# Two-layer encoder on one core: square sums of the set-up taken by ScalarE from a second, token-major input copy, and the third weight pair loaded in the set-up

## The chip, the cores and the metric

One core of one Trainium2 chip runs the program. A core has TensorE (PE, matmuls, with a queue of weight loads, PEld), VectorE (DVE), ScalarE (ACT), GpSimd (POOL) and SyncE (SP), which here issues all DMAs. The metric is the device time of one execution in microseconds; of several executions the median counts.

## The reference, cut to what is computed

The input is 512 tokens of 1024 features, float32. Layer 0 mixes tokens by a gated delta rule (8 heads of 128), layer 1 by a gated linear recurrence, and each is followed by a squared-ReLU MLP with 4096 hidden features. Every part starts with an RMS norm over the features of a token:

```python
def _rmsnorm(x, w):
    xf = x.astype(jnp.float32)
    y = xf * lax.rsqrt(jnp.mean(xf * xf, axis=-1, keepdims=True) + EPS)
    return (y * w.astype(jnp.float32)).astype(x.dtype)
...
proj = y @ w_in                      # 1024 x 4112, split in q, k, v, gate, a, b
qkv = jax.nn.silu(_causal_conv(qkv, conv_w)).astype(f32)
```

The change concerns the first of these norms and the first projections.

## The kernel before

Activations lie feature-major: 8 tiles of 128 features x 512 tokens. A float32 product is made of rounded parts: each weight and each input is split in a high and a low part, and a block of 128 output features takes, for each of the 8 feature tiles k, three matmuls of 512 columns: whi with yh (L125), whi with yl (L126), wlo with yh (L127), 24 in all. Weights come in pairs of blocks, 1 MB of float32 ("raw", two buffers). ScalarE rounds raw to whi (L114) and a second engine subtracts to get wlo (L115). There are three sets of whi and wlo tiles; the third set has tags of its own.

The norm's factor is applied behind the projection: y is only x times the norm's weight, and a projected block is multiplied by the row factors rB afterwards (z, L389, for the heads). So TensorE can start before the square sums are there, and the first use of rB is after the first block.

`setup` (L230 to L262) runs over the feature tiles in steps that end at 1, 2, 4, 6, 8. Each step loads the x tiles (L267), splits each into yh (ScalarE, L216) and yl (VectorE, L219), takes its square on ScalarE (L160, L163) and adds it to the sum sqacc on VectorE or GpSimd (L165); then it loads the step's pieces of the first two weight pairs (L251) and splits them, the first pair's wlo on GpSimd and the second's on VectorE (L252). After the loop come constants, all on SP's queue.

`gdn` (L271 on) loads more constants and gdn_ab, the weights of the decay and gate columns, casts them (L286), and then asks for the first six projected blocks: `stream` makes the first four from the two pairs of the set-up with the loop over k outside (96 matmuls), then loads the third pair and projects its two blocks. With a raised priority, `rstd_rows` turns sqacc into rB: rounded high and low parts, two matmuls "ps" with a column of ones (L195), a wide scaling, Ln and Exp on 128x512, three wide VectorE passes. `gdn_decay` follows with pab (16 matmuls over all y, L335), pt, and small work. Another function, `rstd` (L167), which the second layer uses, goes by a 128x4 tile: small Ln, Exp and VectorE steps to the root rsr, then four broadcasts "pb" through TensorE (L180) and one copy to rB.

The order of the instructions on each engine is fixed when the program is built: a planner takes, by priority, what it reckons to be ready by its own estimate of times. On the chip each engine works through its order and waits where a result is late.

Of the kernel before, what the change touches and what calls it, by code (L numbers as in the profile page):

```python
# [11 lines left out]
F32 = mybir.dt.float32  # L12
F32R = mybir.dt.float32r
U8 = mybir.dt.uint8
AF = mybir.ActivationFunctionType
# [3 lines left out]
T, D, HID, NH, P = 512, 1024, 4096, 8, 128  # L19
NB = D // P  # L20
B = 32
MIX = {"ma": 2, "mb": 3}
NC = T // P
EPS = 1e-6
# [9 lines left out]
class Net:  # L34
# [59 lines left out]
        self.last_switch, self.since_switch = i, []  # L94


    def weight_tiles(self):
        tile = lambda tag, dt, bufs: self.wp.tile([P, NB, 256], dt, tag=tag, bufs=bufs, name=self.name(tag))
        self.nw_tiles += 1

        last = self.nw_tiles % 3 == 0 and not self.two
        return (tile("raw", F32, 2), *(tile(t + "3", F32R, 1) if last else tile(t, F32R, 2) for t in ("whi", "wlo")))

    def weights(self, src):

# [24 lines left out]
    def stream(self, src, y, first=None, wide=0, tokens=slice(0, T), spare=0):  # L130


        n = src.shape[0]
        if wide:
            first = first or [self.weights(src[i]) for i in range(wide)]
            yield from self.project([(w, b) for w in first for b in (0, 1)], y, tokens)
        for i in range(wide, n):
            w = self.weights(src[i])
            for b in (0, 1):
                yield self.project([(w, b)], y, tokens, i - wide < spare)[0]  # L140

# [22 lines left out]
            e = nc.gpsimd if eng == "g" else nc.vector  # L164
            e.tensor_tensor(out=self.sq, in0=self.sq, in1=t, op=ALU.add)  # L165

    def rstd(self):  # L167

        nc = self.nc
        ps = self.mix("ps")  # L170
        for c in range(NC):
            nc.tensor.matmul(ps[:, c:c + 1], lhsT=self.sq[:, c * P:(c + 1) * P], rhs=self.ones,
                             start=True, stop=True)
        x = self.work("rsx", [P, NC])
        nc.vector.tensor_scalar(out=x, in0=ps[:, 0:NC], scalar1=1.0 / D, scalar2=EPS,
                                op0=ALU.mult, op1=ALU.add)
        r = self.rsqrt(x, "rs")
        pb = self.mix("pb")
        for c in range(NC):
            nc.tensor.matmul(pb[:, c * P:(c + 1) * P], lhsT=r[:, c:c + 1].to_broadcast([P, P]),  # L180
                             rhs=self.ident, start=True, stop=True)
        rb = self.work("rB", bufs=2)
        nc.scalar.copy(out=rb, in_=pb)
        return r, rb
# [35 lines left out]
                                       op0=ALU.mult, op1=ALU.subtract)  # L220
        return yh, yl

    def renew(self, c, norm, sq_eng="g", act=False):

        with self.tc.high_priority(offset=3000 if c == NB - 1 else 0):
            self.y[c] = self.split_norm(c, self.nw[:, norm * NB + c:norm * NB + c + 1], act)
            self.square_into(c == 0, self.h[c], sq_eng)


    def setup(self, w):  # L230

        nc = self.nc
        self.table("natural_log_exp_and_others")
        self.h, self.y = [], [None] * NB

        zeros = self.work("gate", bufs=2)
        nc.vector.memset(zeros, 0.0)
        warm = self.mix("warm", [P, WARM])
        for _ in range(2):
            nc.tensor.matmul(warm, lhsT=zeros[:, 0:P], rhs=zeros[:, 0:WARM], start=True, stop=True)  # L240
        pairs = [self.weight_tiles() for _ in (0, 1)]
        start = 0
        for end in (1, 2, 4, 6, 8):
            k = slice(start, end)
            for c in range(start, end):
                self.h.append(self.load_x(c))
                if c == 0:
                    self.nw = self.const("norms", [P, 5 * NB])
                self.renew(c, 0, "g" if c % 2 or c == 0 else "v", act=True)
            for i, (raw, hi, lo) in enumerate(pairs):  # L250
                nc.sync.dma_start(out=raw[:, k], in_=w[i][:, k])  # L251
                self.split_weights(raw, hi, lo, k, (nc.gpsimd, nc.vector)[i])  # L252
            start = end
        self.ident = self.const("ident", [P, P])
        self.ones = self.const("ones", [P, 1])
        self.one = self.cp.tile([P, 1], F32R, tag="one", name="one")
        nc.scalar.copy(out=self.one, in_=self.ones)
        self.tri = self.work("e", [P, P])
        nc.sync.dma_start(out=self.tri, in_=self.a["tri"])
        self.lmask = self.mask("lmask", [P, len(LEVELS) + 1, B])  # L260
        self.ident32 = self.const("ident32", [P, B])
        return [(hi, lo) for _, hi, lo in pairs]  # L262

    def load_x(self, c):
        tag, bufs = (("kd", 3), ("aa", 3), ("n", 2))[c % 3]
# [5 lines left out]
    def gdn(self, first):  # L271
        nc, a = self.nc, self.a
        self.emask = self.const("emask", [P, P])
        self.conv = self.const("conv", [P, 3 * NH, 4])
        self.onorm = self.const("onorm", [P, 1])
        self.pick = self.const("pick", [4 * NH, 2 * NH])
        alog = self.cp.tile([P, NH], F32, tag="alog", name="alog")
        nc.sync.dma_start(out=alog, in_=a["alog"].partition_broadcast(P))
        dtb = self.cp.tile([P, NH], F32, tag="dtb", name="dtb")
        nc.sync.dma_start(out=dtb, in_=a["dtb"].partition_broadcast(P))  # L280

        abraw = self.work("gate", [P, NB, 2 * NH], bufs=2)
        nc.sync.dma_start(out=abraw, in_=a["gdn_ab"])
        ab = self.work("x", [P, NB, 4 * NH], F32R)
        hi = ab[:, :, 0:2 * NH]
        nc.scalar.copy(out=hi, in_=abraw)  # L286
        nc.vector.tensor_tensor(out=ab[:, :, 2 * NH:], in0=abraw, in1=hi.bitcast(F32), op=ALU.subtract)


        blocks = self.stream(a["gdn_in"][0:3 * NH // 2], self.y, first, 2, spare=1)  # L290
        blocks = chain([next(blocks) for _ in range(6)], blocks)
        with self.tc.high_priority(offset=3000):
            self.rb = self.rstd_rows()
            self.gdn_decay(ab, alog, dtb)


        self.two = True
        xa, xb = (self.wp.tile([P, 4, T], F32, tag=t, bufs=1, name=self.name(t)) for t in ("whi3", "wlo3"))
        self.extra = dict(kq=xa[:, 0:2], v=xa[:, 2], kd=xa[:, 3], aa=xb[:, 0], n=xb[:, 1], ot=xb[:, 2], w2=xb[:, 3])
        self.o, self.on = [None] * NH, [None] * NH  # L300
        hd = {0: self.gdn_conv(0, blocks)}
        self.gdn_silu([hd[0]])
        for j in range(NH + 2):
            todo = []
            if j + 1 < NH:
                hd[j + 1] = self.gdn_conv(j + 1, blocks)
                todo.append(hd[j + 1])
            sg = []
            for i in GATES[j]:
                sg += self.gdn_gates(i)  # L310
            with self.tc.high_priority(offset=3000):
                for i in SCANS[j]:
                    self.gdn_scan(i, hd)
                if j < NH:
                    self.gdn_local(j, hd)
                if 2 <= j <= NH and j % 2 == 0:
                    self.gdn_inverse((j - 2, j - 1), hd)
                if todo or sg:
                    self.gdn_silu(todo, sg)
            for h, t in sg:  # L320
                self.gdn_gated(h, t)
        self.nw_tiles, self.two = 0, False
        self.h = [self.load_x(c) for c in range(NB)]
# [656 lines left out]
def layout(x, gdn_w_in, gdn_conv, gdn_a_log, gdn_dt_bias, gdn_onorm, gdn_w_out, hgrn_w_in, hgrn_lb_logits,  # L980
           hgrn_gnorm, hgrn_w_out, norm_mix, norm_mlp, mlp_w_up, mlp_w_down, norm_final):
    i = np.arange(P)
    block = lambda start, h: np.arange(start + h * P, start + (h + 1) * P)
    o = {"x": x[0].T.reshape(NB, P, T).transpose(1, 0, 2)}
    norms = np.stack([norm_mix[0], norm_mlp[0], norm_mix[1], norm_mlp[1], norm_final])
    o["norms"] = norms.reshape(5, NB, P).transpose(2, 0, 1).reshape(P, 5 * NB)
    o["ident"] = np.eye(P, dtype=np.float32)
# [8 lines left out]
    w = gdn_w_in[0]  # L996
# [5 lines left out]
    w = hgrn_w_in[0]  # L1002
# [22 lines left out]
```

## Time and profile before

| | us |
|---|---|
| median of 3 runs (lowest, highest) | 1361.32 (1360.67, 1361.95) |
| the profiled execution | 1360.81 |
| its span, first to last instruction | 1359.0 |
| TensorE busy | 1332.3 |
| VectorE busy | 819.8 |
| ScalarE busy | 546.4 |
| GpSimd busy | 171.9 |
| mean granted TensorE clock | 0.994 |

The profile was taken in one execution; times in it count from the start of the span. A line of the timeline gives the start and duration of an instruction, and in brackets the idle time of its engine before it with what released it. Matmuls are pipelined, so the distance of two starts, not the duration, is what one costs. A clock of 1.00 is full speed, 0.50 the lower of the two levels. Some matmul records can be missing.

### The profile page before, as it was taken

To read this page: it belongs to the slowest core of one execution; us is meant where nothing else is said; L and a number is where in the kernel's file an instruction comes from. 1 tells how busy PE (TensorE), PEld (TensorE's weight loads), DVE (VectorE), ACT (ScalarE), POOL (GpSimd) and SP (SyncE) were. 2 spreads that over 40 slices of the span, in tenths; PEclk is the share of its full clock that TensorE was granted. 3 is DMA by queue.
4 is the path that set the end of the run, shared out by engine and by line. 5 is a ranking of instruction groups with operands and counts; after the bars stand their busy time and mean duration, and the time that the engine had idled before them with its cause. 6 is when DMAs were issued, how large, how long until landed. Compare 5 with 4: busy or idle time off the path is not lost.

```text
span 1359.0 us, 24194 instructions
## 1 busy us (share of the span) xinstructions
PE 1332.3 (98%) x10340; PEld 1101.3 (81%) x10340; DVE 819.8 (60%) x1408; ACT 546.4 (40%) x1016; POOL 171.9 (13%) x172
## 2 busy tenths in 40 slices
PE   7999999999999999999999999999999999999997
PEld 5777777878888888888888888888888888888897
DVE  5896777766844444444483997787674444445453
ACT  5663556454344224132123444545334313214242
POOL 4001021100200120201220010100100020110232
PEclk8999999999999999999999999999999999999999
DMA  6131111222332222232320211121142223232242
GB/s 200 42 115 35 61 64 34 79 79 66 136 109 94 93 93 93 94 102 94 114 93 31 95 64 64 63 94 63 62 155 93 93 94 110 93 108 93 93 140 78
DMA packets 23356, 121.57 MB, mean 89 GB/s; under 512 B 3664, under 2 KB 6864, under 8 KB 9680
## 3 DMA queue, kind: packets, MB, share of 16 engines
q1 hardware_dynamic: 23248, 120.02, 26.2%
q8 instruction: 81, 1.33, 0.4%
q14 instruction: 27, 0.22, 0.0%
HBM read 117.91 MB, written 2.10 MB: 88 GB/s over the span
## 4 chain that ended last, share of the span: by engine, by line
PE 87%; DVE 6%; ACT 4%; issue 1%; DMA 0%; POOL 0%; SPq 0%; POOLq 0%; DVEq 0%; ACTq 0%
PE pj L126 25%; PE pj L125 25%; PE pj L127 25%; PE pga L475 1%; DVE whi L739 1%; PE pj L712 1%; PE pj L711 1%; PE pj L710 1%; ACT whi L114 1%; PE gr L780 1%; PE pu L520 1%; PE px L513 1%; DVE wlo L115 1%; PE pw L590 1%; PE po L826 1%
## 5 line engine op out<-in xcount | busy, mean ns | idle before, releaser
L114 ACT CAST whi<-raw 128x1024 fp32r<-128x1024 f32 (+2 forms) x222 | 221.2, 1023 | 416.0 <-PE pj L126 400.9
L115 DVE TENSOR_TENSOR wlo<-raw,whi 128x1024 fp32r<-128x1024 f32 (+2 forms) x217 | 290.9, 1352 | 153.0 <-ACT whi L114 150.7
L126 PE MATMUL pj<-yl,whi 128*128 128x512 f32 x960 | 382.3, 398 | 0.0
L125 PE MATMUL pj<-yh,whi 128*128 128x512 f32 x960 | 381.2, 397 | 0.8 <-ACT whi L114 0.8
L127 PE MATMUL pj<-yh,wlo 128*128 128x512 f32 x960 | 379.9, 396 | 0.1
L125 PEld LDWEIGHTS pj<-yh,whi 128*128 128x128 f32 x960 | 181.8, 189 | 38.2 <-ACT whi L114 2.5
L127 PEld LDWEIGHTS pj<-yh,wlo 128*128 128x128 f32 x960 | 181.2, 189 | 36.1 <-POOL wlo L115 0.5
L126 PEld LDWEIGHTS pj<-yl,whi 128*128 128x128 f32 x960 | 181.8, 189 | 34.9
L126 PE MATMUL pj<-ol,whi 128*128 128x512 f32 x336 | 131.2, 391 | 0.0
L886 DVE TENSOR_TENSOR gate<-pj,rB 128x512 f32<-128x512 f32 x56 | 38.6, 691 | 148.2 <-PE pj L127 148.2
L127 PE MATMUL pj<-oh,wlo 128*128 128x512 f32 x320 | 125.0, 391 | 0.0
L125 PE MATMUL pj<-oh,whi 128*128 128x512 f32 x320 | 125.0, 391 | 0.0
L872 ACT ACTIVATE z<-pj 128x512 f32<-128x512 f32 x64 | 38.0, 594 | 113.6 <-PE pj L127 109.6
L888 POOL TENSOR_TENSOR kd<-kd,gate 128x512 f32<-128x512 f32 x18 | 23.3, 1293 | 462.2 <-DVE gate L886 462.2
L126 PEld LDWEIGHTS pj<-ol,whi 128*128 128x128 f32 x336 | 63.2, 188 | 12.8
L125 PEld LDWEIGHTS pj<-oh,whi 128*128 128x128 f32 x320 | 60.2, 188 | 12.3
L127 PEld LDWEIGHTS pj<-oh,wlo 128*128 128x128 f32 x320 | 60.0, 188 | 12.3
L127 PE MATMUL pj<-kq,wlo 128*128 128x512 f32 (+1 forms) x192 | 67.8, 355 | 0.5 <-DVE wlo L115 0.5
L125 PE MATMUL pj<-kq,whi 128*128 128x512 f32 (+1 forms) x192 | 68.0, 354 | 0.0
L126 PE MATMUL pj<-kq,whi 128*128 128x512 f32 (+1 forms) x192 | 67.9, 354 | 0.0
L165 POOL TENSOR_TENSOR sqacc<-sqacc,z 128x512 f32<-128x512 f32 x25 | 38.8, 1553 | 223.7 <-ACT z L163 219.6
L739 DVE TENSOR_TENSOR whi<-whi 128x256 f32<-128x256 f32 x112 | 49.2, 441 | 6.3 <-ACT whi L742 4.7
(379 smaller groups left out, 1942.0 us busy)
## 6 DMA issues: line engine op xcount, KB each, us to landing
raw<-down SPq DMA_DIRECT2D x36, 1024.0 KB, 4.9
raw<-up SPq DMA_DIRECT2D x32, 1024.0 KB, 4.8
raw<-gdn_in SPq DMA_DIRECT2D x14, 1024.0 KB, 4.8
raw<-hgrn_fq SPq DMA_DIRECT2D x8, 1024.0 KB, 4.9
raw<-gdn_out SPq DMA_DIRECT2D x4, 1024.0 KB, 5.4
raw<-hgrn_i SPq DMA_DIRECT2D x4, 1024.0 KB, 4.9
raw<-hgrn_gate SPq DMA_DIRECT2D x4, 1024.0 KB, 4.9
raw<-hgrn_out SPq DMA_DIRECT2D x4, 1024.0 KB, 4.9
```

Of the source, the lines that this page charges most:

```text
L114: self.nc.scalar.copy(out=hi[:, k], in_=raw[:, k])
L115: eng.tensor_tensor(out=lo[:, k], in0=raw[:, k], in1=hi[:, k].bitcast(F32), op=ALU.subtract)
L125: mm(o, lhsT=hi[:, k, c], rhs=yh, start=(k == 0), stop=False)
L126: mm(o, lhsT=hi[:, k, c], rhs=yl, start=False, stop=False)
L127: mm(o, lhsT=lo[:, k, c], rhs=yh, start=False, stop=(k == NB - 1))
L165: e.tensor_tensor(out=self.sq, in0=self.sq, in1=t, op=ALU.add)
L475: mm(pga[:, c - c2], lhsT=ck(k, c), rhs=kq[:, :, c * P:(c + 1) * P], start=True, stop=True)
L513: mm(px[b, a, c], lhsT=n[a][b, c, b], rhs=wd[b, a, c], start=True, stop=True, tile_position=(b.start, b.start))
L739: mul = lambda o, x, y: nc.vector.tensor_tensor(out=o, in0=x, in1=y, op=ALU.mult)
L872: nc.scalar.activation(out=z, in_=out, func=AF.Relu)
L886: nc.vector.tensor_tensor(out=t, in0=out, in1=self.r2b, op=ALU.mult)
L888: e.tensor_tensor(out=self.h[c], in0=self.h[c], in1=t, op=ALU.add)
```

## The change

`setup` no longer squares the feature-major tiles. The host hands over the input a second time as xt, token-major: 4 chunks of 128 tokens x 1024 features. Each chunk is loaded (512 KB each, one after the pieces of step 4, one after step 6, two after step 8) into a free kq buffer, and ScalarE squares it with its accumulator, which leaves one column of the 128x4 tile sums. The row factors then come from `rstd(self.sums)[1]` in place of `rstd_rows()`; with sums given, `rstd` skips its ps matmuls. Both pairs' wlo are split by VectorE. Behind ident, `setup` also loads the third weight pair in four pieces of 256 KB into free ol buffers and splits them into the third set of whi and wlo; `stream` takes it as ready, so that pair uses no raw buffer. sqacc, its additions on GpSimd and VectorE, and GpSimd's splits are gone from the set-up.

```diff
-    def weight_tiles(self):
+    def weight_tiles(self, raw=True):
...
+        split = [tile(t + "3", F32R, 1) if last else tile(t, F32R, 2) for t in ("whi", "wlo")]
+        return [tile("raw", F32, 2)] + split if raw else split
...
+        first = first or [self.weights(src[i]) for i in range(wide)]
         if wide:
-            first = first or [self.weights(src[i]) for i in range(wide)]
-            yield from self.project([(w, b) for w in first for b in (0, 1)], y, tokens)
+            yield from self.project([(w, b) for w in first[0:wide] for b in (0, 1)], y, tokens)
         for i in range(wide, n):
-            w = self.weights(src[i])
+            w = first[i] if i < len(first) else self.weights(src[i])
...
-    def rstd(self):
+    def rstd(self, sums=None):
         nc = self.nc
-        ps = self.mix("ps")
-        for c in range(NC):
-            nc.tensor.matmul(ps[:, c:c + 1], lhsT=self.sq[:, c * P:(c + 1) * P], rhs=self.ones,
-                             start=True, stop=True)
+        if sums is None:
+            sums = self.mix("ps")
+            for c in range(NC):
+                nc.tensor.matmul(sums[:, c:c + 1], lhsT=self.sq[:, c * P:(c + 1) * P], rhs=self.ones,
+                                 start=True, stop=True)
         x = self.work("rsx", [P, NC])
...
         pairs = [self.weight_tiles() for _ in (0, 1)]
+        self.sums = self.cp.tile([P, NC], F32, tag="sums", name="sums")
         start = 0
-        for end in (1, 2, 4, 6, 8):
+        for end, chunks in ((1, ()), (2, ()), (4, (0,)), (6, (1,)), (8, (2, 3))):
             k = slice(start, end)
             for c in range(start, end):
                 self.h.append(self.load_x(c))
                 if c == 0:
                     self.nw = self.const("norms", [P, 5 * NB])
-                self.renew(c, 0, "g" if c % 2 or c == 0 else "v", act=True)
+                self.y[c] = self.split_norm(c, self.nw[:, c:c + 1], act=True)
             for i, (raw, hi, lo) in enumerate(pairs):
                 nc.sync.dma_start(out=raw[:, k], in_=w[i][:, k])
-                self.split_weights(raw, hi, lo, k, (nc.gpsimd, nc.vector)[i])
+                self.split_weights(raw, hi, lo, k, nc.vector)
+            for c in chunks:
+                t = self.work("kq", [P, 2 * T], bufs=4)
+                nc.sync.dma_start(out=t, in_=self.a["xt"][:, c])
+                nc.scalar.activation(out=t, in_=t, func=AF.Square, accum_out=self.sums[:, c:c + 1])
             start = end
         self.ident = self.const("ident", [P, P])
+        third = self.weight_tiles(raw=False)
+        for i in range(0, NB, 2):
+            raw = self.work("ol", [P, 2, 256], bufs=NH)
+            nc.sync.dma_start(out=raw, in_=w[2][:, i:i + 2])
+            self.split_weights(raw, *(t[:, i:i + 2] for t in third), slice(0, 2), nc.vector)
         self.ones = self.const("ones", [P, 1])
...
-        return [(hi, lo) for _, hi, lo in pairs]
+        return [(hi, lo) for _, hi, lo in pairs] + [third]
...
-            self.rb = self.rstd_rows()
+            self.rb = self.rstd(self.sums)[1]
             self.gdn_decay(ab, alog, dtb)
...
-    o = {"x": x[0].T.reshape(NB, P, T).transpose(1, 0, 2)}
+    o = {"x": x[0].T.reshape(NB, P, T).transpose(1, 0, 2), "xt": x[0].reshape(NC, P, D).transpose(1, 0, 2)}
```

## Rows read from the trace of the kernel before

**Rows 1.** The page of the profiled execution: busy time by engine.

```profile
PE 1332.3 (98%) x10340; PEld 1101.3 (81%) x10340; DVE 819.8 (60%) x1408; ACT 546.4 (40%) x1016; POOL 171.9 (13%) x172
```

**Rows 2.** TensorE's waits over the span: waiter, awaited, us in total, times, longest.

```profile
PE ps L195 <- ACT one L257: 5.3, 1, 5.3
...
PE pb L935 <- DVE rsr L153: 1.4, 1, 1.4
```

**Rows 3.** Timeline at 13 to 25 us: start, us, engine, line, operation, [idle before].

```profile
13.12 0.19 PEld L127 LDWEIGHTS pj<-yh,wlo 128*128 128x128 f32 x1 [0.48 <-POOL wlo L115]
...
18.43 1.59 POOL L165 TENSOR_TENSOR sqacc<-sqacc,z 128x512 f32<-128x512 f32 x1 [0.69 <-DVE sqacc L165]
18.47 0.39 PE L126 MATMUL pj<-yl,whi 128*128 128x512 f32 x1
...
18.70 0.39 PE L127 MATMUL pj<-yh,wlo 128*128 128x512 f32 x1
18.82 1.76 DVE L219 SCALAR_TENSOR_TENSOR yl<-kd,norms,yh 128x512 fp32r<-128x512 f32 x1
...
20.49 0.74 DVE L219 SCALAR_TENSOR_TENSOR yl<-aa,norms,yh 128x512 fp32r<-128x512 f32 x1
...
21.84 0.68 DVE L115 TENSOR_TENSOR wlo<-raw,whi 128x512 fp32r<-128x512 f32 x1
21.98 1.66 POOL L165 TENSOR_TENSOR sqacc<-sqacc,z 128x512 f32<-128x512 f32 x1 [1.96 <-DVE both L380]
...
24.43 0.79 PE L195 MATMUL ps<-z,one 128*128 128x512 f32 x1 [5.35 <-ACT one L257]
```

**Rows 4.** Groups by line and shape, 0 to 25 us: count, busy us, mean ns.

```profile
L125 PE MATMUL pj<-yh,whi 128*128 128x512 f32 x17 | 7.5, 451 | 0.8 <-ACT whi L114 0.8
...
L114 ACT CAST whi<-raw 128x512 fp32r<-128x512 f32 x6 | 3.5, 606 | 0.0
...
L163 ACT ACTIVATE z<-kd 128x512 f32<-128x512 f32 x2 | 1.2, 625 | 0.0
```

**Rows 5.** TensorE in a stretch: length, busy (instructions), granted clock, DMA share, GB/s.

```profile
24.43:28.86 4.43, 4.43 (x10) 0.50 0.67 222
```

**Rows 6.** Timeline at 28 to 41 us: ab's cast, first pab, first z.

```profile
28.62 0.28 ACT L286 CAST x<-gate 128x128 fp32r<-128x128 f32 x1
...
31.49 0.39 PE L335 MATMUL pab<-yh,x 128*32 128x512 f32 x1
...
40.47 0.69 DVE L389 TENSOR_TENSOR z<-pj,rB 128x512 f32<-128x512 f32 x1 [0.86 <-PE pj L127]
```

**Rows 7.** Timelines at 719 and 49 us: root and pb; a ScalarE activation of 128x1024.

```profile
719.07 0.16 DVE L175 TENSOR_SCALAR rsx<-ps 128x4 f32<-128x4 f32 x1 [1.21 <-PE ps L172]
...
720.37 1.14 PE L180 MATMUL pb<-ident,rsr 128*128 128x128 f32 x8
...
49.32 1.06 ACT L85 ACTIVATE kq<-kq 128x1024 f32<-128x1024 f32 x1
```

**Rows 8.** SP's timeline; issues (KB, us to landing), 0 to 60 us; stretches, columns as above.

```profile
10.37 1.06 SPq L251 DMA_DIRECT2D raw<-gdn_in  x2
...
18.48 0.35 SPq L283 DMA_DIRECT2D gate<-gdn_ab  x1
...
raw<-gdn_in SPq DMA_DIRECT2D x6, 256.0 KB, 5.5
...
gate<-gdn_ab SPq DMA_DIRECT2D x1, 64.0 KB, 2.3
...
4.00:5.00 1.00, 0.38 (x1) 0.00 (x0) 0.15 (x1) 1.00 (x3) 0.00 (x0) 1.00 0.81 250
...
14.00:15.00 1.00, 1.00 (x6) 0.82 (x5) 1.00 (x3) 1.00 (x3) 0.64 (x1) 1.00 1.05 404
```

**Rows 9.** TensorE's timeline at 103 us; stretches of all engines (PE, PEld, DVE, ACT, POOL).

```profile
103.51 0.39 PE L520 MATMUL pu<-ud,xd 32*32 32x32 f32 x23 [2.08 <-issue]
...
60.00:80.00 20.00, 20.00 (x96) 16.50 (x95) 19.54 (x51) 13.62 (x34) 2.67 (x2) 1.00 0.31 106
```

More of the change, by code (lines that the diff above doesn't have):

```diff
@@ L101, in weight_tiles @@
         last = self.nw_tiles % 3 == 0 and not self.two
-        return (tile("raw", F32, 2), *(tile(t + "3", F32R, 1) if last else tile(t, F32R, 2) for t in ("whi", "wlo")))
+        split = [tile(t + "3", F32R, 1) if last else tile(t, F32R, 2) for t in ("whi", "wlo")]
+        return [tile("raw", F32, 2)] + split if raw else split
     def weights(self, src):
@@ L165, in square_into @@
             e.tensor_tensor(out=self.sq, in0=self.sq, in1=t, op=ALU.add)
-    def rstd(self):
+    def rstd(self, sums=None):
         nc = self.nc
-        ps = self.mix("ps")
-        for c in range(NC):
-            nc.tensor.matmul(ps[:, c:c + 1], lhsT=self.sq[:, c * P:(c + 1) * P], rhs=self.ones,
-                             start=True, stop=True)
+        if sums is None:
[3 more added lines that the diff above has]
+                                 start=True, stop=True)
         x = self.work("rsx", [P, NC])
-        nc.vector.tensor_scalar(out=x, in0=ps[:, 0:NC], scalar1=1.0 / D, scalar2=EPS,
+        nc.vector.tensor_scalar(out=x, in0=sums[:, 0:NC], scalar1=1.0 / D, scalar2=EPS,
                                 op0=ALU.mult, op1=ALU.add)
@@ L221, in split_norm, with renew @@
         return yh, yl
-    def renew(self, c, norm, sq_eng="g", act=False):
+    def renew(self, c, norm, sq_eng="g"):
         with self.tc.high_priority(offset=3000 if c == NB - 1 else 0):
-            self.y[c] = self.split_norm(c, self.nw[:, norm * NB + c:norm * NB + c + 1], act)
+            self.y[c] = self.split_norm(c, self.nw[:, norm * NB + c:norm * NB + c + 1])
             self.square_into(c == 0, self.h[c], sq_eng)
```

## The prediction, made before the change was run

> **What bounds the kernel now.** I read the page first. TensorE is busy for 1332.3 of 1359.0 us; VectorE, the next, for 60% of them [rows 1]. So the end is set by TensorE's time: a microsecond taken from its idle or slow stretches comes off the end if what follows is released by TensorE too. Its idle time is 26.7 us, and I asked for its waits next, over the whole run. The longest is one wait of 5.3 us, in front of the first "ps" matmul of L195 [rows 2]. The stage to look at is therefore the set-up.
>
> The timeline of that stretch [rows 3] shows the chain behind the wait. By then 51 projection matmuls are recorded, 17 of L125 [rows 4] and as many of L126 and L127; the last starts at 18.70. In the steady rows one starts 0.228 us after the other (18.47, 18.70), so the next was due at 18.93. It started at 24.43, 5.50 us late, because TensorE's in-order queue had the two ps matmuls next. These need the sum of squares: VectorE's yl of 1.76 us and its next of 0.74, then GpSimd's last addition of 1.66 us at 21.98. GpSimd is the slow member: its 1.66 stand against 0.63 of ScalarE's square of the same size [rows 4] and 0.68 of VectorE's split at 21.84. The wait costs twice: the granted clock, 1.00 from 14 to 15 us [rows 8], falls to the lower of its two levels during it, and the ten matmuls from 24.43 to 28.86 run at 0.50, 1.2 GHz [rows 5]. They take 4.43 us for 10 x 0.228 = 2.28, so 2.15 lost, and 0.09 more on the next.
>
> Does a gain here reach the end? VectorE's first work on projected heads (z, L389) starts at 40.47, right after TensorE's last pass over that block [rows 6]. The later stage is released by TensorE, so it should move as a whole.
>
> **The change part by part, on the path.** The sum goes by the profiled execution, span 1359.0 and 1360.81 in all; the median of the runs is 1361.32, 0.5 more, and I take differences off the median.
>
> Removed: (a) the wait for the square sums, 5.50; (b) the half-clock stretch it leaves, 2.15 + 0.09 = 2.24; (c) the two ps matmuls, 2 x 0.228 = 0.46 (their slow form is in b); (d) TensorE's weight load's 0.48 us wait for GpSimd's split at 13.12 [rows 3], which delays the next matmuls by some 0.3, since VectorE does that split. Together 8.5.
>
> Added on TensorE: four broadcasts "pb" of the 128x4 root. The same function runs later in the kernel: 1.14 us for its eight passes [rows 7]. I take 1.1; if they slip between other matmuls less, never below zero, as they are real passes. Net 7.4.
>
> Added waits. pb needs the root. The last weight piece was issued with the pair at 10.37 and took 5.5 us to land [rows 8], so about 16.6. Ahead of the root there are now four copies of 512 KB, 2.10 MB: 5.2 us at the 404 GB/s of 14 to 15 us, 8.4 at the 250 of 4 to 5 [rows 8]. The last copy lands at 21.8 to 25.0. ScalarE squares one in about 1.3 us: no square of that shape with an accumulated sum is in the trace; an activation of 128x1024 takes 1.06 [rows 7], and I add a quarter for the sum (its bounds: nothing, and as much again). The root's chain, from rsx to the first pb, took 1.3 us later in the kernel [rows 7]. So the root is there at about 24.4, at worst 27.6. Unhindered TensorE, at 18.6 after 51 or 52 matmuls, has some 25 more behind it by 24.4 and reaches the end of the first block (35 more, and pab, pt) near 33. Where in its queue pb stands I can't see; this bounds its wait between 0 and the 5.50 + 2.24 of today. I take 1.4 us, the row of the same dependency elsewhere, TensorE's pb waiting for rsr [rows 2], because the order before held no wait of that size but where GpSimd ran late.
>
> Hidden, with their cover. (1) The copies also come ahead of weights: 0.52 MB ahead of pieces 4 and 5 is 1.3 us (2.1 at 250 GB/s), 1.05 MB ahead of the last is 2.6 (4.2). The last pieces land at 19.2 (20.8); two roundings of 0.61 and a split of 0.68 [rows 4] make 21.1 (22.7), and TensorE wants that split at about 23.6, 22 matmuls after 18.6. Cover 2.5 us; with none, each microsecond late costs one. (2) ScalarE loses eight squares and the three 128x512 passes of the old root, 11 x 0.63 = 6.9, and gains four of 1.3 = 5.2 and smaller ones; it was gapless and stays so, nothing on the path. (3) VectorE loses three additions and the root's five wide passes, gains the five splits that were GpSimd's, three of 0.68 and two of half the size, under 3.4: less work than before, and shorter instructions. Rows: yl took 1.76 with GpSimd active and 0.74 without [rows 3]. The Trainium skill ("SBUF — State Buffer", Who interferes with whom) says that a VectorE instruction with two SBUF inputs waits out a GpSimd instruction that reads SBUF. By that, all splits run at the short row, and the last ones end at 21.1 as in (1). If the slowing were VectorE's own, a split of 1.76 would end at 22.2, still inside that cover. (4) The third pair's four pieces, split in 4 x 0.61 on ScalarE and 4 x 0.68 on VectorE, work that stood later in the set-up before. TensorE needs it after the first four blocks, near 34; it lands by about 25 to 29. Nothing. (5) SP's queue gains eight issues of some 0.35 us [rows 8]. Behind them stand the constants and the gdn_ab load, issued at 18.48 and landed 2.3 us later, at 20.8 [rows 6, 8]. 3.15 MB more at 404 GB/s is 7.8, so gdn_ab is there at about 28, cast and split 28.6. Who waits: pab, 16 matmuls, which stood at 31.49 with some 20 projections between ps and it [rows 6]. This is the second new wait, and a rival. (6) The next pair's load waited for GpSimd's last split to free its tile and can only be earlier.
>
> Sum: 5.50 + 2.24 + 0.46 + 0.3 - 1.1 - 1.4 = 6.0 us. 1361.32 - 6.0 = 1355.3.
>
> The Trainium skill ("DMA: Bandwidth & Descriptors", Specifications) puts the limit of HBM for a core at about 358 GB/s, and speaks against a second copy of the input. The trace shows 404 from 14 to 15 us [rows 8], so it disagrees; by 358 the copies would take 5.9 us and the root come 0.7 later, inside the bound above.
>
> **The rivals.** *A new wait in the old place.* pab keeps its position, 20 projections behind the ps place, and TensorE gets there at 18.6 + 4.6 + 1.1 = 24.3 while gdn_ab's split is ready at 28.6: a wait of 4.3, and perhaps the clock with it (2.2). The gain shrinks to 8.5 - 1.1 - 4.3 = 3.1, or 0.9: 1358.2 to 1360.4. For it: the loads in front on SP are certain. Against: ScalarE's order has the gdn_ab cast behind both exponentials (28.62, [rows 6]) although the load had landed at 20.8, as if the order reckoned with late loads; it would then move pab back.
> *Slower.* pb stands where ps stands, at 18.6, and the copies come at 250 GB/s: the root is there at 27.6, a wait of 9.0, and 2.24 of slow clock, 11.2 against the 7.4 saved: 3.8 slower, 1365.1. At 404 GB/s it is 8.0 against 7.4, about the time of now; it decides from a root later than 23.8. Against it: the order can see that the root needs more loads than the sums did.
> *The stop before 103.5 us.* TensorE stood 2.1 us for nothing that the profile shows, in front of L520's matmuls at 103.51 [rows 9]. If the slow clock behind it costs as after the first stop, some 2, it is worth 4 in all. A shifted load may miss it, and the time would be 1351.3; or another may be hit so, 1359.3.
> *Nothing gained.* The wait is hidden anyway because VectorE, 19.5 of 20 us busy from 60 to 80 [rows 9], sets the pace: speaks against it that z at 40.47 waits for TensorE and that TensorE is busy all of those 20 us. The time would stay at 1361.3.
>
> **How the numbers follow.** Forecast 0.58, with an own range of 1353.9 (no new wait) to 1357.0. The new wait at pab 0.17, the stop missed 0.08 or doubled 0.04, nothing gained 0.05, slower 0.08. The range must keep 8 in 10: from the missed stop, 1351.3, to just above the pab wait with the clock, 1360.6. What a measurement can tell here is 0.2%, 2.7 us: faster means under 1358.6. Faster: 0.58 + 0.08 + 0.11 of the pab case, 0.77. Same: the rest of that case, the doubled stop, nothing gained, 0.15. Slower 0.08.
>
> **What would show it.** Right: no GpSimd additions or splits before 24 us, VectorE's splits at 0.68, the clock at 1.00 from 20 to 30 us, TensorE busy from 10 to 40, z of L389 starting near 34.5 (40.47 - 6.0), and the rest of the span as long as before, about 1318.5 from there. Wrong: a wait before pb or pab of over 3 us (the first or second rival), a wait for whi of the last pieces (cover (1) gone), or z early and the gain lost between 40 and 130 us (the order of the heads' stage, or the stop).

## The result, and the profile after

The changed kernel takes 1363.34 us (median of 20 runs, 1362.49 to 1367.19) where the kernel before, timed beside it, takes 1361.3 (20 runs, 1359.45 to 1364.67): a ratio of 1.0018, 95% interval 1.0012 to 1.0025. It is 2.0 us slower, where 6.0 us faster was forecast. The profiled execution took 1364.64 us, 1.3 above that median; its span is 1362.8 us, 3.8 longer than before.

The set-up did become what the forecast said. TensorE in stretches (columns: length; PE, PEld, DVE, ACT and POOL busy with their instructions; granted clock; DMA share; GB/s):

```profile
10.00:20.00 10.00, 10.00 (x46) 8.28 (x45) 5.56 (x9) 7.80 (x13) 0.00 (x0) 1.00 1.03 390
20.00:30.00 10.00, 10.00 (x50) 8.43 (x49) 5.32 (x13) 6.25 (x15) 1.03 (x2) 1.00 0.65 194
...
40.00:50.00 10.00, 10.00 (x52) 8.21 (x51) 7.65 (x23) 5.64 (x12) 0.30 (x1) 1.00 0.00 1
50.00:60.00 10.00, 6.41 (x32) 4.96 (x31) 9.46 (x28) 8.77 (x29) 0.00 (x0) 0.87 0.01 2
60.00:70.00 10.00, 5.89 (x19) 4.40 (x18) 9.10 (x18) 4.79 (x9) 1.26 (x1) 0.50 0.14 32
70.00:80.00 10.00, 10.00 (x45) 8.32 (x44) 9.00 (x34) 8.73 (x28) 1.30 (x1) 0.94 0.46 178
```

From 10 to 50 us TensorE doesn't stop and its clock stays at 1.00; the wait of [rows 2] and the half-clock stretch of [rows 5] are gone. Then it stands for 7.7 us between 50 and 70, and its clock falls to 0.50. The first two lines of its waits (waiter, awaited, us in total, times, longest) name the place:

```profile
PE pk L450 <- ACT kq L85: 4.3, 2, 4.1
PE pga L489 <- ACT x L85: 2.8, 1, 2.8
```

pk and pga belong to the first work on the heads (`gdn_local`). Both wait for ScalarE, and ScalarE waits for VectorE: ahead of pk for its convolutions, which make kq, ahead of pga for a small result on k. VectorE's timeline back from there, to where it begins with the heads:

```profile
26.30 1.29 DVE L116 TENSOR_TENSOR wlo<-ol,whi 128x512 fp32r<-128x512 f32 x2
30.59 0.29 DVE L301 TENSOR_TENSOR x<-gate,x 128x128 fp32r<-128x128 f32 x1 [3.00 <-ACT x L300]
34.50 1.23 DVE L116 TENSOR_TENSOR wlo<-raw,whi 128x1024 fp32r<-128x1024 f32 x1 [3.62 <-ACT whi L115]
38.85 0.68 DVE L351 TENSOR_TENSOR z<-pab,rB 32x512 f32<-32x512 f32 x1 [3.12 <-PE pab L349]
39.46 0.67 DVE L403 TENSOR_TENSOR z<-pj,rB 128x512 f32<-128x512 f32 x1
41.67 0.19 DVE L358 TENSOR_TENSOR ab_a<-pt,dtb 128x32 f32<-128x32 f32 x1 [1.55 <-PE pt L354]
```

The first z on a head starts at 39.46, only 1.0 us before that of [rows 6], though rB was there at 30.27:

```profile
29.68 0.59 ACT L186 COPY rB<-pb 128x512 f32<-128x512 f32 x1 [2.98 <-PE pb L183]
30.27 0.29 ACT L300 CAST x<-gate 128x128 fp32r<-128x128 f32 x1
```

In VectorE's order there stand, ahead of the heads, gdn_ab's split, half a split of the fourth weight pair and the product on pab. It waits for each, and of the 11 us from 28 to 39 it works 1.67 (5.93 before):

```profile
28.00:39.00 11.00, 11.00 (x54) 7.92 (x53) 1.67 (x3) 3.93 (x6) 0.13 (x1) 1.00 0.56 198
```

The product on pab waits for TensorE, but TensorE did not stop for gdn_ab. That load's split was done at 30.88, and pab began at 34.95, in its place behind 118 projections (70 in the kernel before):

```profile
34.95 0.39 PE L349 MATMUL pab<-yh,x 128*32 128x512 f32 x1
```

gdn_ab is late as forecast: SP issues its load at 27.64 (18.48 in [rows 8]):

```profile
27.64 0.35 SPq L297 DMA_DIRECT2D gate<-gdn_ab  x1
```

So the late load acts in part by itself and in part through the later place that the planner then gave pab (behind 88 projections in f1 below, where the load comes early); no run separates the two.

And the decay's chain (ab_a, ab_gc and on), of which in the kernel before all but the last step was done ahead of the first convolution (at 43.48), now falls between the heads' convolutions. So kq of head 1 is later than before, not earlier. First the kernel before, then the one after, ScalarE's silu of that kq:

```profile
63.73 1.06 ACT L85 ACTIVATE kq<-kq 128x1024 f32<-128x1024 f32 x1 [2.08 <-DVE kq L393]
```

```profile
65.83 1.06 ACT L85 ACTIVATE kq<-kq 128x1024 f32<-128x1024 f32 x1 [3.98 <-DVE kq L407]
```

Before, this silu ended at 64.79 and pk of head 1 began at 64.91 on TensorE, which had stood for only 0.1 us since 30: the two engines arrived in step. Now TensorE loses nothing in the set-up and VectorE begins with the heads only 1.0 us earlier, so TensorE is early at pk and stands there.

### The profile page after: what moved, and what is told of

It reads as the page before. It is cut to its first block, busy times and chain, and to the rows that moved or that the text cites. A ratio compares the mean times of both kernels' runs of the same rounds, so it can differ in the third digit from the quotient of the medians.

```text
span 1362.8 us, 24203 instructions
## 1 busy us (share of the span) xinstructions
PE 1334.3 (98%) x10346; PEld 1103.7 (81%) x10346; DVE 813.5 (60%) x1411; ACT 546.5 (40%) x1018; POOL 155.3 (11%) x163
## 4 chain that ended last, share of the span: by engine, by line
PE 86%; DVE 7%; ACT 5%; issue 1%; DMA 0%; POOL 0%; POOLq 0%; SPq 0%; DVEq 0%; ACTq 0%
PE pj L128 25%; PE pj L127 25%; PE pj L126 25%; PE pga L489 1%; DVE whi L753 1%; PE pj L725 1%; PE pj L724 1%; PE pj L726 1%; PE gr L794 1%; DVE kq L407 1%; ACT L91 1%; ACT whi L115 1%; DVE wlo L116 1%; PE pu L534 1%; PE pw L604 1%
## 5 line engine op out<-in xcount | busy, mean ns | idle before, releaser
L115 ACT CAST whi<-raw 128x1024 fp32r<-128x1024 f32 (+2 forms) x220 | 219.3, 1024 | 415.3 <-PE pj L127 398.2
L166 POOL TENSOR_TENSOR sqacc<-sqacc,z 128x512 f32<-128x512 f32 x21 | 32.4, 1544 | 220.9 <-ACT z L164 220.8
```

The source lines that it names most:

```text
L115: self.nc.scalar.copy(out=hi[:, k], in_=raw[:, k])
```

## The experiments

Every kernel is placed by two numbers read from its trace and order: when VectorE starts the first z, and how many projection matmuls (pj) stand ahead of head 1's pk in TensorE's order. "Lost" is TensorE's idle time plus its busy time times (1 - granted clock), added up from windows of 1 us.

| kernel | gdn_ab issued | first z | pj ahead of pk | pk of head 1 | lost 10:50 | lost 50:80 | lost 80:350 | median us |
|---|---|---|---|---|---|---|---|---|
| before | 18.5 | 40.47 | 174 | 64.9 | 7.7 | 0.1 | 6.6 | 1361.3 to 1362.2 |
| after | 27.6 | 39.46 | 174 | 66.9 | 0.0 | 11.7 | 4.0 | 1363.3 |
| e4_one_square | 19.2 | 33.05 | 174 | 57.5 | 0.4 | 0.4 | 6.9 | 1354.5 |
| f1_ab_before_third | 17.2 | 32.31 | 186 | 59.2 | 1.4 | 0.5 | 6.3 | 1355.4 |
| e2_squares_only | 23.9 | 36.20 | 150 | 62.5 | 1.2 | 12.1 | 3.2 | 1364.2 |
| e3_third_pair_only | 21.5 | 39.52 | 174 | 66.9 | 7.5 | 1.8 | 3.7 | 1360.3 |
| g1_split4_first | 27.5 | 38.45 | 194 | 66.7 | 0.6 | 8.7 | 5.6 | 1361.2 |
| g2_f1_split4_late | 17.5 | 32.61 | 186 | 59.5 | 0.0 | 1.4 | 3.5 | 1351.7 |
| g3_e2_split_first | 25.7 | 35.99 | 202 | 62.6 | 0.6 | 4.1 | 8.9 | 1361.0 |
| h1_f1_split_first | 17.0 | 32.70 | 189 | 60.5 | 0.0 | 0.1 | 7.0 | 1356.5 |
| i1_conv_first | 27.2 | 30.45 | 201 | 63.3 | 0.0 | 0.1 | 7.3 | 1356.9 |
| i4_h1_first_z_late | 16.9 | 42.81 | 194 | 63.9 | 0.0 | 7.3 | 4.0 | 1359.6 |
| i2_f1_conv_first | 18.0 | 27.92 | 194 | 60.5 | 0.4 | 0.2 | 7.3 | 1358.1 |

The three lost columns account for most of the differences: the median less their sum lies between 1346 and 1350.5 in every row, while the medians themselves lie 12.5 us apart. What is left, some 4 us, is more than the 2.0 us of the change itself, in part because the losses are those of one execution and the time is the median of several. So the table sorts these kernels, but it can't tell 2 us.

**Theories at first.** A: the late gdn_ab load. B: the order of the heads' instructions, which the planner makes anew. C: VectorE sets the pace of the heads' stage and takes up any lead of TensorE. Four kernels: the changed one with gdn_ab's load ahead of the third pair's pieces; the one before with only the first tile squared; and each half of the change alone.

*f1_ab_before_third*, from the changed kernel:

```diff
+        self.abraw = self.work("gate", [P, NB, 2 * NH], bufs=2)
+        nc.sync.dma_start(out=self.abraw, in_=self.a["gdn_ab"])
         third = self.weight_tiles(raw=False)
...
-        abraw = self.work("gate", [P, NB, 2 * NH], bufs=2)
-        nc.sync.dma_start(out=abraw, in_=a["gdn_ab"])
+        abraw = self.abraw
```

> The changed kernel with one load moved: gdn_ab is issued ahead of the third pair's pieces instead of behind them and eleven constants. Theory A (the changed kernel lost its gain because the decay columns came 9 us later, and with them the start of the heads' chain on VectorE and ScalarE): gdn_ab is issued near 17 us instead of 27.64, pab starts by 29 instead of 34.95, the first z of L403 by 33 instead of 39.46, pk of head 0 by 46 instead of 51.93, TensorE's waits between 50 and 70 us fall from 7.7 to under 2, and the time is 1357 (1355 to 1359.5). Theory B (the waits at 55 to 68 us come from another order of the heads' instructions, whatever the decay): pab is early, the waits stay, 1362 to 1364. Theory C (VectorE's work on the heads sets the pace and takes up any lead): pk early, but the time within 1 us of the kernel before, 1360.3 to 1362.3.

Measured: 1355.4 us, ratio 0.9951 (0.9939 to 0.9964). This one move turns 2.0 us lost into 6.8 won against the kernel before timed beside it (1362.2), near the 6.0 that were forecast for the change. pab starts at 27.70 in place of 34.95, the first z at 32.31, and the stop is gone, which B did not expect. SP's issue, VectorE's first z, and a stretch:

```profile
17.17 0.33 SPq L265 DMA_DIRECT2D gate<-gdn_ab  x1
...
32.31 1.27 DVE L404 TENSOR_TENSOR z<-pj,rB 128x512 f32<-128x512 f32 x2
...
50.00:60.00 10.00, 10.00 (x50) 8.39 (x49) 9.94 (x27) 6.38 (x12) 1.29 (x1) 1.00 0.15 62
```

*e4_one_square*, from the kernel before:

```diff
-                self.renew(c, 0, "g" if c % 2 or c == 0 else "v", act=True)
+                self.y[c] = self.split_norm(c, self.nw[:, c:c + 1], True)
+                if c == 0:
+                    self.square_into(True, self.h[0])
```

> The kernel before with only the first feature tile squared: seven of the eight squares and all additions are left out, so the norm's factor is not the reference's. gdn_ab stays where it was, landed at 20.8. This is the size of the prize: TensorE's wait of 5.3 us at 18.9 us and the slow clock behind it go, nothing else is loaded later. Theory A and my prediction's sum: the first z near 33 us, the time 1354 to 1356. Theory C: the first z as early, but at least 1360.

Measured: 1354.48 us, ratio 0.9952 (0.9937 to 0.9967). The wait at ps is worth 7.7 us when it goes, so C as put, that any lead is taken up, falls. What this kernel has and the changed one lacks is a first z that moves along, 33.05 against 40.47, and waits for TensorE as before:

```profile
33.05 0.69 DVE L391 TENSOR_TENSOR z<-pj,rB 128x512 f32<-128x512 f32 x1 [0.87 <-PE pj L127]
```

*e2_squares_only*, from the changed kernel:

```diff
-        third = self.weight_tiles(raw=False)
-        for i in range(0, NB, 2):
-            raw = self.work("ol", [P, 2, 256], bufs=NH)
-            nc.sync.dma_start(out=raw, in_=w[2][:, i:i + 2])
-            self.split_weights(raw, *(t[:, i:i + 2] for t in third), slice(0, 2), nc.vector)
...
-        return [(hi, lo) for _, hi, lo in pairs] + [third]
+        return [(hi, lo) for _, hi, lo in pairs]
```

> The changed kernel without the early third pair (it is loaded by the stream as before): 1 MB and four issues less in front of gdn_ab. Theory A: gdn_ab issued near 24 instead of 27.64, pk of head 0 about 2 us earlier than 51.93, time 1360 to 1362.5. Theory B says nothing of it; the waits may fall anywhere.

Measured: 1364.23 us, ratio 1.0020 (1.0011 to 1.0029). This missed what A expected. Here the first z is 4.3 us earlier than before, and still TensorE stands for 8.0 us after 50, in front of pk, pga and pv.

*e3_third_pair_only*: the kernel before, with the five lines that e2 takes out put in, and with what they need in `weight_tiles` and `stream`.

> The kernel before with the early third pair alone; squares, additions and GpSimd's splits stay. The ps matmuls still need GpSimd's sums, near 24 to 26 us, but stand behind more projections, so the wait at 18.9 us shrinks to 2 to 3 us and the clock may stay up; gdn_ab is issued some 3 us later than 18.48. Theory A: first z within 1 us of before, a gain only of what the wait loses if the heads start earlier: 1359 to 1361.5. If the third pair's early work is what matters, 1357 or less.

Measured: 1360.31 us, ratio 0.9985 (0.9974 to 0.9996). The wait at ps stays (4.4 us; 2 to 3 had been expected), and little changes: the harm is not in the early third pair by itself.

**Theory D.** In e2 only 150 projections stand ahead of pk, because the next pair's low halves (wlo) come behind the heads' work in VectorE's order (61.83; in the changed kernel 66.32 and 68.11). So perhaps TensorE stops for want of a split weight pair. g1 and g3 put that pair's subtractions ahead in the changed kernel and in e2, h1 does so in f1, and g2 puts the second of them late in f1. The edit of g1 (g3 and h1 have the same, in g3 for the second call):

```diff
-        for i in (0, 1):
-            self.split_weights(raw, hi, lo, slice(4 * i, 4 * i + 4), nc.vector)
+        self.n_weights = getattr(self, "n_weights", 0) + 1
+        with self.tc.high_priority(offset=6000 if self.n_weights == 1 else 0):
+            for i in (0, 1):
+                self.split_weights(raw, hi, lo, slice(4 * i, 4 * i + 4), nc.vector)
```

> The changed kernel with one thing moved: the two subtractions that split the fourth weight pair (wlo, 128x1024 each, 1.2 us) are put ahead in VectorE's order, before the heads' convolutions; gdn_ab's load stays late, at about 27.6 us on SP. In the changed kernel the first of them ran at 34.50, the others at 66.32 and 68.11, behind the work of heads 0 and 1, and TensorE, which had used up the first three pairs, waited in front of pk and pga for 8 us between 50 and 68. Theory D (the stop is TensorE's lack of a fourth pair): both subtractions before 45 us, TensorE busy for more than 19 of the 20 us from 50 to 70 at a clock of 1.00, and 1355 to 1358.5 us in all, though gdn_ab is as late as before. Theory A (the late gdn_ab load and what depends on it): the stop stays, 1361.5 to 1364. Theory C (VectorE's pace takes up any lead): the splits are only exchanged for convolutions, 1361 to 1364.

Measured: 1361.23 us, ratio 0.9991 (0.9981 to 1.0000). Both subtractions ran at 34.42, and 20 more projections, worth 20 x 0.228 = 4.6 us, stood ahead of pk. The loss shrank by 3.0 us and no more; D had expected it gone, and the time lies 0.3 below A's range and in C's. TensorE waits at the same place for the same kq, in its waits up to 80 us

```profile
PE pk L452 <- ACT kq L85: 4.7, 1, 4.7
```

and in the stretch from 60 to 70 us (columns as above):

```profile
60.00:70.00 10.00, 5.28 (x20) 4.22 (x21) 9.92 (x21) 8.04 (x22) 1.27 (x1) 0.79 0.00 0
```

VectorE is busy for 9.92 of these 10 us: it is not idle work that is missing, it is a late start. A missing weight pair sets how long TensorE has other work, not when kq is ready.

The edit of g2, from f1 (conv_end is the last step of a head's convolutions):

```diff
+        self.n_weights = getattr(self, "n_weights", 0) + 1
...
-            self.split_weights(raw, hi, lo, slice(4 * i, 4 * i + 4), nc.vector)
+            s = self.split_weights(raw, hi, lo, slice(4 * i, 4 * i + 4), nc.vector)
+            if self.n_weights == 1 and i == 1:
+                self.after(s, self.conv_end)
...
```

> The reverse: the kernel with gdn_ab's load issued early (1355.4 us measured) in which only the second subtraction of the fourth pair is ordered behind head 1's last convolution step on VectorE, about where the changed kernel has it. Theory D: TensorE runs out of projections and stops between 50 and 70 for 4 to 8 us, with the clock falling behind it, 1359 to 1364 us. Theory A: gdn_ab is early, so nothing is lost, 1354.5 to 1356.5.

Measured: 1351.70 us, ratio 0.9924 (0.9912 to 0.9937), the fastest of all, and 2.8 below A's range. The loss that D expected did not come: with the first z at 32.61, a subtraction at 58.77 or 62.45 does no harm. It is no clean test of D, since the new order put half of the fifth pair's split in the place, so that again 186 projections stand ahead of pk. Against f1 it gains 3.7 us, and 3.4 of them are a stop at 323 us (1.7 us in front of pt, and as much slow clock) that f1's order has and this one has not. That part of the gain is an accident of the order.

> The kernel with the squares' part of the change alone (third pair split as before; 1364.2 us measured, with waits of 8.0 us between 50 and 80), in which the subtractions of the next weight pair are put ahead in VectorE's order. Theory D: the waits in front of pk, pga and pv shrink below 2 us together, 1356 to 1359.5 us. A or C: 1362.5 to 1365.

Measured: 1360.98 us, ratio 0.9989 (0.9980 to 0.9999). The loss at 50 to 80 us shrinks, from 12.1 to 4.1, with 202 projections in place of 150 (52 x 0.228 = 11.9 us of work), but other losses at 150 to 350 us, of 8.8 (2.6 in e2), take most of it back; the time stays above what D expected.

> Both cures at once: gdn_ab's load ahead of the third pair's pieces and the fourth pair's subtractions ahead in VectorE's order. In the kernel with the early load alone they already ran right after the first z, at 45.0, and TensorE lost only 0.5 us there, so theory D expects nothing more: 1354 to 1357 us, the same as with the early load alone (1355.4). If it gained over 3 us, something else of the early stage is still held by the fourth pair; if it lost as much, the convolutions that are pushed back are worth more than D says.

Measured: 1356.52 us, ratio 0.9959 (0.9946 to 0.9973): as f1, within what can be told.

**Theory E.** The stop is kq's time less TensorE's. kq of head 1 is ready, and its pk starts, some 24 to 28 us behind VectorE's first z in all kernels up to here; TensorE comes when it has worked off what stands ahead of pk. The late gdn_ab matters because VectorE's queue stands behind it. This and A differ where gdn_ab is late and the heads don't stand behind it (i1), and where it is early and they start late (i4).

*i1_conv_first*, from the changed kernel (i2: the same from f1):

```diff
             self.rb = self.rstd(self.sums)[1]
+            hd = {0: self.gdn_conv(0, blocks)}
             self.gdn_decay(ab, alog, dtb)
...
-        hd = {0: self.gdn_conv(0, blocks)}
         self.gdn_silu([hd[0]])
```

> The changed kernel with head 0's products z and convolutions written ahead of the decay's work, so that they stand in VectorE's queue before the product on pab; gdn_ab's load stays as late as in the changed kernel. There VectorE's first z on the heads came at 39.46, behind its wait for pab (3.1 us, until 38.85), and head 1's kq was through ScalarE's silu at 66.9, some 27 us after the first z, as in the other kernels (23 to 27). Theory E (the stop is the time at which VectorE begins with the heads; the late load acts only because VectorE's queue stands behind it): first z at 30.5 to 32, head 1's kq at 56 to 60, TensorE's idle and slow time from 50 to 80 under 3 us together, 1355 to 1358.5 us. Theory A (the late load itself holds TensorE, through pab and the decay's chain): the stop stays, 1361 to 1364.

Measured: 1356.88 us, ratio 0.9958 (0.9942 to 0.9974). gdn_ab is as late as in the changed kernel, and nothing is lost between 50 and 80 us but 0.1, which A does not allow. SP's issue of its load, VectorE's products on the heads and on pab, and two stretches:

```profile
27.24 0.35 SPq L297 DMA_DIRECT2D gate<-gdn_ab  x1
```

```profile
30.45 1.89 DVE L403 TENSOR_TENSOR z<-pj,rB 128x512 f32<-128x512 f32 x3 [3.29 <-ACT rB L186]
...
41.49 0.68 DVE L351 TENSOR_TENSOR z<-pab,rB 32x512 f32<-32x512 f32 x1 [0.61 <-PE pab L349]
```

```profile
50.00:60.00 10.00, 10.00 (x51) 8.14 (x50) 9.70 (x30) 8.49 (x30) 0.00 (x0) 1.00 0.33 107
60.00:70.00 10.00, 9.94 (x51) 7.96 (x50) 9.00 (x31) 9.79 (x28) 1.30 (x1) 1.00 0.00 0
```

Its nearest neighbour is g1: the load late in both, the fourth pair split before 41 us in both, 194 against 201 projections. The largest difference left is the first z, at 38.45 or at 30.45, and the loss is 8.7 or 0.1. kq of head 1 came later than I had put it, at 63.1, behind a decay chain that starts later, but TensorE had work until then. So 8.0 us at the first z are 3.4 at pk of head 1 (66.7 and 63.3); of the 4.7 us that TensorE stands there in g1 these are the larger part, and the rest is that TensorE, with 7 projections more, comes later. The first z alone doesn't set the stop; kq does.

*i4_h1_first_z_late*, from h1:

```diff
-        nc.vector.tensor_tensor(out=low, in0=prow[B:2 * B], in1=low.bitcast(F32), op=ALU.subtract)
+        self.decay_end = nc.vector.tensor_tensor(out=low, in0=prow[B:2 * B], in1=low.bitcast(F32), op=ALU.subtract)
...
-            nc.vector.tensor_tensor(out=z, in0=next(blocks), in1=self.rb, op=ALU.mult)
+            first = nc.vector.tensor_tensor(out=z, in0=next(blocks), in1=self.rb, op=ALU.mult)
+            if j == 0 and i == 0:
+                self.after(first, self.decay_end)
```

> The reverse: the kernel with gdn_ab's load early and the fourth pair's subtractions ahead (1356.5 us measured, first z at 32.7, no stop between 50 and 80), in which head 0's first product z is ordered behind the last VectorE instruction of the decay, so that VectorE begins with the heads at about 38 to 41. Theory E: head 1's kq is ready 25 to 27 us later, at 64 to 67, TensorE, with 194 projections ahead of it, is there by about 61 and stops for 3 to 6 us, and 1 to 2.5 of slow clock follow: 1360 to 1364. Theory A (gdn_ab is early, so nothing is lost): 1355.5 to 1357.5. Theory D (the fourth pair is early, so nothing is lost): the same.

Measured: 1359.60 us, ratio 0.9980 (0.9969 to 0.9991), 3.1 us slower than h1 (the slowest run of h1, 1357.45, lies below the fastest of this kernel, 1357.89). The load is early, the fourth pair is split at 39.72, the first z is late, and the stop is back, with the clock behind it. VectorE's first z, TensorE's longest wait from 40 to 80 us, and a stretch:

```profile
42.81 1.89 DVE L406 TENSOR_TENSOR z<-pj,rB 128x512 f32<-128x512 f32 x3
```

```profile
PE pk L455 <- ACT kq L85: 3.0, 2, 2.8
```

```profile
60.00:70.00 10.00, 6.05 (x24) 3.97 (x23) 9.25 (x25) 8.54 (x25) 1.16 (x1) 0.75 0.00 0
```

The loss at 50 to 80 us is 7.3, against 0.1 in h1, and neither A nor D allows it. The median is 0.4 below the range that I gave for E: the first z came still later than I had put it (42.8 for 38 to 41), but with the decay out of the way kq followed it in 21 us, not 25.

> The kernel with gdn_ab's load early (1355.4 us) and head 0's products and convolutions ahead of the decay's work as well. Theory E: there is no stop left between 50 and 80 to be taken away (0.5 us there), so VectorE's earlier start is worth nothing: 1352 to 1357, apart from the small stops at 150 and 320. If it came to 1349 or less, the heads' stage would follow VectorE's start all the way.

Measured: 1358.10 us, ratio 0.9970 (0.9954 to 0.9985), 1.1 above what was expected, with runs from 1354.9 to 1361.2 and a profiled span of 1354.9. In its trace nothing is lost between 50 and 80, so an earlier first z (27.92) is worth nothing more. Its profiled execution, 1356.7 us, is as long as f1's, 1356.6; why its median lies above f1's is open.

## Why the prediction was wrong

The steps on the set-up held in the main. The ps wait, the slow stretch behind it and the ps matmuls are gone. pb took 1.05 (1.1 forecast) at 28.59, and TensorE waited for neither pb nor pab; the 1.4 and the rival's 4.3 us there cost nothing, because the order put pb behind 94 projections and pab behind 118, where ps had 51 and pab 70. A square took 1.06 and its accumulator read 0.19, 1.25 for 1.3. The root was there at 26.4, 2.0 behind the forecast and inside its bound of 27.6: the last square began at 23.05, and the root's chain took 2.1 us for 1.3, with splits of the third pair between its steps. ScalarE was not gapless, as item (2) had it: it worked 9.19 of the 10 us from 10 to 20 before and 7.80 after, when it waited for the copies. VectorE's splits of 128x512 took 0.69 and all its yl 0.75, where some of [rows 3] took 1.76 beside GpSimd. With the rule of the Trainium skill ("SBUF — State Buffer", Who interferes with whom) that the prediction weighed, the trace agrees. From 10 to 20 us the loads came at 390 GB/s, near the 404 of [rows 8]. With the limit of about 358 GB/s of the Trainium skill ("DMA: Bandwidth & Descriptors", Specifications) the trace disagrees. gdn_ab was issued at 27.64 and took 2.5 us to land; its split was done at 30.88, for the forecast 28.6. The prediction's own terms make 18.48 + 7.8 + 2.3 = 28.6 for the landing; it booked that figure for the finished split too.

The step that failed is the one under "Does a gain here reach the end?": "The later stage is released by TensorE, so it should move as a whole." It rested on one row, the first z at 40.47, which ends a wait of 0.86 us for TensorE [rows 6]. That row says who came last in the kernel before, not who comes last when the change delays another. Where nothing else is delayed the step holds: in e4 the first z moved by 7.4 us. In the changed kernel z stood behind rB, at 30.3, and the product on pab, which could start at 38.85, so that it moved by 1.0 us, not by 6.0. The step asked what is late next for TensorE and not for VectorE.

Item (5) had the facts for it: gdn_ab late, pab its consumer. It priced the lateness only as TensorE's wait at pab. But pab's product also stands ahead of the heads' z in VectorE's order, and z, with all its inputs there at 30.3, began 9 us later, behind it. The rival "A new wait in the old place" had the right load and the wrong engine. The rival "Nothing gained" had the right engine, from the same 19.54 of 20 us [rows 9], and was given 5 in 100 because z waited for TensorE, the same reading again. "Slower" ended on the right side by a mechanism that did not occur: pb cost no wait.

The sum, put right by the lost time of the two kernels: 7.7 taken away in the set-up (forecast 5.50 + 2.24 = 7.74), 11.7 in place of 0.1 between 50 and 80 (forecast: no change), and 2.6 less from 80 to 350. Most of the last is luck: the stop before 103.5 us, which the rival had at 4 and which measured 2.1 + 1.7 = 3.8 with its clock, is not there in the changed kernel, and no run shows why. Over 10 to 350 us the lost time goes from 14.5 to 15.7, 1.2 more. pb less the two ps adds 1.05 - 0.46 = 0.6. Together 1.8, near the 2.0 of the medians; the two profiled executions lie 3.8 apart, of which 1.2 more are lost time outside 10 to 350 us and some 0.8 can't be traced.

The point "z early and the gain lost between 40 and 130 us" was named among what would prove the forecast wrong. It was lost there, with z not early.

## What to carry to other kernels

A wait on the bounding engine may be time that another engine needs for its own chain, and then it only moves. Before booking its removal, follow the next meeting of the two engines (here pk of head 1, where kq's silu ended 0.12 us ahead of it) and ask when the other engine can start: each instruction in front in its queue, with its inputs, however small. A load pushed back in a queue is to be priced at every engine whose order stands behind its consumer, and the cure may be one line of order (f1, i1), not the change itself.

## What the runs showed that I had not expected

Small moves at 20 us change what happens far behind: the stop of 2.1 us for nothing that the profile shows [rows 9] appears at 96 to 104 us in the kernel before and in e4, at 150 us in others (1.86 in g3, 1.63 in h1), and in the changed kernel there is no such stop of over 0.3 us up to 350. No run here shows what it comes from. A stop of TensorE can cost more than its length: 1.7 us at 323 in f1 took 1.7 more by a clock of 0.50 behind it, the 7.7 of the changed kernel took 4.0, and the 1.63 at 151 in h1 took none.
